# Weight tiles 64 and 96 bytes longer: moving the buffers of the split weights against the other operands in SBUF

## The chip, the cores and the metric

The kernel runs on one core of one Trainium2 chip. The metric is the device time of one execution in microseconds (us). The kernel before takes 2689.38 us, the median of 3 runs that lie between 2688.95 and 2689.45 us.

In what follows a matrix multiplication on TensorE is a *matmul*: one operand, the *weights* (128 columns here), is loaded into the array by an instruction of its own, the *weight load*; the other, the *moving* operand (up to 512 columns), streams past it, and the result is added up in a PSUM bank. The load of the next matmul's weights runs while the present matmul streams.

## The reference

A two-layer encoder trunk on 256 tokens of width 2048, in float32. Per layer:

```python
u = rmsnorm(x, norm_mix[l])
c_q, c_kv, k_pe, q_na, k_na, v_na, gate_a, gate_b = split(u @ w_in[l])      # 2048 x 8256
q  = (rmsnorm(c_q,  norm_qa[l])  @ w_uq[l])     # low-rank query and key/value of MLA
kv = (rmsnorm(c_kv, norm_kva[l]) @ w_ukv[l])
y_a = mla_attention(...) @ w_o_mla[l]           # 8 heads
y_b = neighbourhood_attention(...) @ w_o_na[l]  # 8 heads, windowed, with a bias
x = x + (sigmoid(gate_a) * y_a + sigmoid(gate_b) * y_b) @ w_out[l]
h = rmsnorm(x, norm_mlp[l]) @ w_ff1[l]          # 2048 -> 8192
x = x + square(relu(h)) @ w_ff2[l]              # 8192 -> 2048
```

and a last RMSNorm. Nearly all of the arithmetic is in the products of 256 rows with large weight matrices.

## The kernel before

**Two halves instead of float32.** Each float32 operand is split into `hi` (the value rounded to fp32r, a form that TensorE streams fast) and `lo` (what is left over, in fp32r too). A product is then hi·hi + hi·lo + lo·hi. Activations lie in *pairs*: one tile of 128 x 512 fp32r whose left 256 columns are the hi half and whose right 256 are the lo half. Weights come in by DMA as `raw` tiles (L167, 1 MB each, issued by SyncE), ScalarE casts them into a `hi` tile (L172), and VectorE subtracts to get the `lo` tile (L173). A `hi` or `lo` tile is 128 partitions x 1024 words, that is 4096 bytes in each partition, and holds two blocks of 128 x 512 of the weight matrix. There are four buffers for `hi` and four for `lo` (`HBUFS`), used in turn, three for `raw`.

**Two forms of product.** `gemm_b` (helper `mm_b`, L194 and L195) has the weight matrix in the array: the pair streams past a block of `hi` (512 columns, L194), then its left half past the same block of `lo` (256 columns, L195). `gemm_a` (helper `mm_a`, L199 to L201) has the activations in the array: `hi` streams past the pair's left block (L199), `lo` past the same block (L200), `hi` past the pair's right block (L201), 512 columns each. `gemm_b` makes q, k, the latents and the first half of the MLP; `gemm_a` the gates, the output projections and the second half of the MLP. A third helper, `mm_3` (L204 to L206), does the scores and the value products of the attention heads with 256 streaming columns. In the profile's names `bank<-pair,hi` reads: into a PSUM bank, moving operand pair, weights hi.

**What sets the order.** Each engine runs its list in program order; the tile framework puts the lists together with a timeline of its own, and starts an instruction where its buffers come free. Heads, rotations and transposes are generators that `tick` feeds in between the matmuls of the large products (`SPACING`, `LAG1`, `LAG2`). The ring `small` (8 buffers of 128 x 256) holds what `whole` (L210, L212) takes out of PSUM after a `gemm_b`, and a few short-lived tiles of the attention part.

**Where tiles lie.** Within a partition the pools stand one behind the other, and in a pool the buffers of one name: constants, the two `xt` tiles, `raw` (3 x 8192 bytes), `hi` (4 x 4096), `lo` (4 x 4096), the 44 slots of 2048 bytes (all pairs, and the value tiles `vh`, `vl`), then the small ones. In the built program every `raw`, `hi`, `lo` and slot buffer begins at a multiple of 256 bytes; `small` begins 64 bytes past one, and `pp`, the probabilities of a head that stream in the value product (L204 to L206, `abank<-pp,pair` and `abank<-pp,vh`), 192 bytes past one. The *distance* of a weight load below is the start of the tile that is loaded minus the start of the tile that streams meanwhile, modulo 256 bytes (the slices inside tiles begin at multiples of 512 bytes and change nothing in it). Before the change it is 0 for all loads of `mm_b` and `mm_a` and for the scores, and 64 for the loads beside a streaming `pp`.

Of the kernel before, what the change touches and what calls it, by code (L numbers as in the profile page):

```python
# [28 lines left out]
F32R = mybir.dt.float32r  # L29
# [4 lines left out]
P = 128  # L34
# [18 lines left out]

NSLOT, ABANKS, SMALL, RBUFS, HBUFS = 44, 3, 8, 3, 4


SPACING, LAG1, LAG2 = 6, 13, 3
# [3 lines left out]
def trunk(ctx: ExitStack, tc: tile.TileContext, x, w_in, w_uq, w_ukv, rpb, w_o_mla, w_o_na,  # L63
# [3 lines left out]
    wpool = ctx.enter_context(tc.tile_pool(name="wpool", bufs=4))  # L67
# [89 lines left out]
    def weights(w, nk, c0, n, before=None):  # L157


        step = 2 if before else 4  # L160
        for k0 in range(0, nk, 2):
            if before:
                before(k0)
            if k0 % step == 0:
                raw = wpool.tile([P, 2048], F32, tag="raw", name="raw", bufs=RBUFS)
                raw = raw[:, :step * n].rearrange("p (k n) -> p k n", n=n)
                nc.sync.dma_start(raw, w[k0 * P:(k0 + step) * P, c0:c0 + n].rearrange("(k p) n -> p k n", p=P))  # L167
            hi = wpool.tile([P, 1024], F32R, tag="hi", name="hi", bufs=HBUFS)
            lo = wpool.tile([P, 1024], F32R, tag="lo", name="lo", bufs=HBUFS)
            hi, lo = (t[:, :2 * n].rearrange("p (k n) -> p k n", n=n) for t in (hi, lo))  # L170
            src = raw[:, k0 % step:k0 % step + 2]
            nc.scalar.copy(hi, src)  # L172
            nc.vector.tensor_tensor(lo, src, hi.bitcast(F32), op=ALU.subtract)  # L173
            yield k0, hi, lo

    def weights_twice(w, nk, c0, n):

        raw = wpool.tile([P, 2048], F32, tag="raw", name="raw", bufs=RBUFS)
        raw = raw[:, :nk * n].rearrange("p (k n) -> p k n", n=n)
        nc.sync.dma_start(raw, w[:nk * P, c0:c0 + n].rearrange("(k p) n -> p k n", p=P))  # L180
        for k0 in range(0, nk, 8):
            hi = wpool.tile([P, 1024], F32R, tag="hi", name="hi", bufs=HBUFS)
            lo = wpool.tile([P, 1024], F32R, tag="lo", name="lo", bufs=HBUFS)
            hi, lo = (t.rearrange("p (k e n) -> p k e n", e=2, n=n) for t in (hi, lo))
            src = raw[:, k0:k0 + 8]
            for e in range(2):
                nc.scalar.copy(hi[:, :, e], src)
                nc.vector.tensor_tensor(lo[:, :, e], src, hi[:, :, e].bitcast(F32), op=ALU.subtract)
            hi, lo = (t.rearrange("p k e n -> p k (e n)") for t in (hi, lo))
            yield k0, hi, lo  # L190
# [24 lines left out]
    def gemm_a(w, c0, acts, evac):  # L215

        nk = len(acts)
        ps = [bank() for _ in range(2)]
        for k0, wh, wl in weights(w, nk, c0, 512):
            for t in range(2):  # L220
                for k in range(k0, k0 + 2):
                    mm_a(ps[t], have(acts, k), t, wh[:, k - k0], wl[:, k - k0], k == 0, k == nk - 1)
                tick()
        for t in range(2):
            evac(t, ps[t])

    def gemm_b(w, c0, acts, evac, before=None, ahead=None):

        nk = len(acts)
        ps = [bank() for _ in range(4)]  # L230
        for k0, wh, wl in weights(w, nk, c0, 512, before):
            for m in range(4):
                ms = slice(m * P, (m + 1) * P)
                for k in range(2):
                    mm_b(ps[m], wh[:, k, ms], wl[:, k, ms], have(acts, k0 + k), k0 + k == 0, k0 + k == nk - 1)
                tick()
        if ahead:
            ahead()
        for m in range(4):
            evac(m, ps[m])  # L240
# [234 lines left out]
    for l in range(DEPTH):  # L475
# [11 lines left out]
        for g in range(2):  # L487
            qn, kn = [None] * 4, [None] * 4
            gemm_b(wi, C_QN + g * 512, xg, to_pair(mix, qn), enter if l == g == 0 else None,
                   scaled if g == 0 else None)  # L490
            gemm_b(wi, C_KN + g * 512, xg, to_pair(mix, kn))
            ps = [bank() for _ in range(2)]
            for k0, wh, wl in weights(wi, NC, C_VN + g * 512, 512):
                for t in range(2):
                    for k in range(k0, k0 + 2):
                        mm_a(ps[t], xg[k], t, wh[:, k - k0], wl[:, k - k0], k == 0, k == NC - 1)
                    tick()
                    tick()
            vt = [values(ps[t], mix.col, t) for t in range(2)]
            for j in range(4):  # L500
                h = g * 4 + j
                queued.append(na_head(l, h, qn[j], kn[j], vt, setter(att_na, h)))
# [17 lines left out]
        for k0, wh, wl in weights_twice(wi, NC, C_KPE, ROPE):  # L520
            for k in range(8):
                mm_b(ps, wh[:, k], wl[:, k], xg[k0 + k], k0 + k == 0, k0 + k == NC - 1)
# [208 lines left out]
```

## Time and profile before

| | |
|---|---|
| median of 3 runs | 2689.38 us |
| the profiled execution: its own time | 2689.91 us |
| its span in the trace | 2688.1 us |
| TensorE busy with matmuls | 2666.8 us, 13596 instructions |
| weight loads | 2268.7 us, 13596 instructions |
| VectorE busy | 1602.9 us |
| ScalarE busy | 1277.1 us |

The span is 1.8 us shorter than the execution's own time, which also holds what lies around it. In the trace matmuls overlap: a matmul of 512 columns is recorded with some 390 ns, though the next one begins well before those are over. How fast the stream really runs is therefore read from the distance between the starts of neighbouring matmuls, or from how many of them begin in a window of known length, and not from the mean duration of one.

### The profile page before, as it was taken

How to read it: one execution, taken by the hardware profiler on the slowest of the kernel's cores; microseconds unless marked ns; L12 is line 12 of the kernel's file. 1: busy time of each engine (PE TensorE's matmuls, PEld its weight loads, DVE VectorE, ACT ScalarE, POOL GpSimd, SP SyncE). 2: the span in 40 equal slices, each digit the busy share in tenths (PEclk: the TensorE clock that was granted, in tenths of full speed). 3: DMA queues.
4: the chain of work that ended last, by engine and by line, in shares of the span. 5: the costliest groups of instructions: out<-in, count | busy, mean ns of one | idle time of the engine just before them, and what ended most of it. 6: DMA issues, size and time to landing. Idle time of an engine off the chain costs nothing.

```text
span 2688.1 us, 34037 instructions
## 1 busy us (share of the span) xinstructions
PE 2666.8 (99%) x13596; PEld 2268.7 (84%) x13596; DVE 1602.9 (60%) x2158; ACT 1277.1 (48%) x1815; POOL 60.5 (2%) x86
## 2 busy tenths in 40 slices
PE   8999999999999999999999999999999999999998
PEld 7888888888888888888888888888888888888886
DVE  5676486555655546556567754955556555565554
ACT  5554465444434434444445544644444344443443
POOL 1110000000000000000001100000000000000000
PEclk9999999999999999999999999999999999999999
DMA  7555644555565555555555555455555555655554
GB/s 231 184 165 189 195 161 155 189 184 180 186 203 186 190 190 186 197 193 189 183 183 179 171 187 183 153 167 188 188 188 188 189 187 194 208 189 193 188 188 141
DMA packets 253839, 496.49 MB, mean 185 GB/s; under 512 B 12688, under 2 KB 16784, under 8 KB 253680
## 3 DMA queue, kind: packets, MB, share of 16 engines
q1 hardware_dynamic: 250624, 488.14, 55.2%
q0 software_dynamic: 2048, 4.56, 0.6%
q8 instruction: 106, 1.74, 0.3%
q10 hardware_dynamic: 1008, 1.61, 0.2%
q14 instruction: 53, 0.43, 0.0%
HBM read 492.18 MB, written 2.10 MB: 184 GB/s over the span
## 4 chain that ended last, share of the span: by engine, by line
PE 84%; issue 14%; DVE 1%; DMA 1%; ACT 0%; POOL 0%; SPq 0%; POOLq 0%; DVEq 0%; ACTq 0%
PE bank L194 21%; PE bank L199 16%; PE bank L200 16%; PE bank L201 16%; PE bank L195 11%; DMA raw<-in_w_in 1%; PE abank L206 1%; PE abank L205 1%; PE abank L204 1%; PE abank L326 1%; PE abank L377 0%; DVE lo L173 0%; DVE wide L670 0%; PE abank L347 0%; ACT hi L172 0%
## 5 line engine op out<-in xcount | busy, mean ns | idle before, releaser
L173 DVE TENSOR_TENSOR lo<-raw,hi 128x1024 fp32r<-128x1024 f32 (+1 forms) x928 | 1132.5, 1222 | 977.8 <-ACT hi L172 973.0
L172 ACT CAST hi<-raw 128x1024 fp32r<-128x1024 f32 (+1 forms) x928 | 971.8, 1049 | 1131.1 <-PE bank L201 736.2
L194 PE MATMUL bank<-pair,hi 128*128 128x512 f32 x3008 | 1059.0, 398 | 2.3 <-DVE small L212 1.0
L200 PE MATMUL bank<-lo,pair 128*128 128x512 f32 (+1 forms) x2240 | 866.1, 387 | 0.0
L199 PE MATMUL bank<-hi,pair 128*128 128x512 f32 (+1 forms) x2240 | 865.8, 388 | 0.0
L201 PE MATMUL bank<-hi,pair 128*128 128x512 f32 (+1 forms) x2240 | 865.8, 387 | 0.0
L195 PE MATMUL bank<-pair,lo 128*128 128x256 f32 x3008 | 835.5, 280 | 0.4 <-DVE lo L173 0.3
L194 PEld LDWEIGHTS bank<-pair,hi 128*128 128x128 f32 x3008 | 563.5, 188 | 133.0 <-ACT hi L172 1.9
L195 PEld LDWEIGHTS bank<-pair,lo 128*128 128x128 f32 x3008 | 567.7, 189 | 5.9 <-DVE lo L173 1.6
L201 PEld LDWEIGHTS bank<-hi,pair 128*128 128x128 f32 x2240 | 420.8, 188 | 84.6
L199 PEld LDWEIGHTS bank<-hi,pair 128*128 128x128 f32 x2240 | 420.8, 188 | 84.1
L200 PEld LDWEIGHTS bank<-lo,pair 128*128 128x128 f32 x2240 | 420.9, 188 | 82.6
L150 ACT ACTIVATE pair<-small 128x256 fp32r<-128x256 f32 x200 | 73.6, 413 | 89.8 <-DVE small L641 67.1
L210 ACT COPY small<-bank 128x256 f32<-128x256 f32 x218 | 78.6, 369 | 29.0 <-PE bank L195 27.8
L152 DVE TENSOR_TENSOR pair<-small,pair 128x256 fp32r<-128x256 f32 x200 | 76.6, 418 | 19.2 <-ACT pair L150 19.2
L212 DVE TENSOR_TENSOR small<-bank,small 128x256 f32<-128x256 f32 x218 | 83.0, 416 | 0.2
L259 POOL TENSOR_TENSOR col<-var,mhalf 128x2 f32<-128x2 f32 x9 | 6.3, 702 | 1928.8 <-DVE var L257 1928.8
L619 DVE SCALAR_TENSOR_TENSOR xt<-bank,sq,xt 128x512 f32<-128x512 f32 x64 | 45.0, 744 | 7.8 <-PE bank L201 7.8
L641 DVE SCALAR_TENSOR_TENSOR small<-small 128x256 f32<-128x256 f32 x128 | 48.2, 418 | 0.0
L154 DVE SCALAR_TENSOR_TENSOR pair<-abank,g_sb,pair 128x256 fp32r<-128x256 f32 x64 | 29.2, 478 | 23.0 <-ACT pair L150 23.0
L150 ACT ACTIVATE pair<-abank,g_sb 128x256 fp32r<-128x256 f32 x64 | 28.2, 469 | 27.3 <-PE abank L326 23.4
L150 ACT ACTIVATE pair<-abank 128x256 fp32r<-128x256 f32 x64 | 23.6, 381 | 29.2 <-PE abank L206 19.1
(96 smaller groups left out, 789.9 us busy)
## 6 DMA issues: line engine op xcount, KB each, us to landing
raw<-in_w_ff SPq DMA_DIRECT2D x256, 1024.0 KB, 5.0
raw<-in_w_in SPq DMA_DIRECT2D x124, 1024.0 KB, 5.1
raw<-in_w_out SPq DMA_DIRECT2D x32, 1024.0 KB, 4.9
raw<-in_w_o_na SPq DMA_DIRECT2D x16, 1024.0 KB, 4.9
raw<-in_w_o_mla SPq DMA_DIRECT2D x16, 1024.0 KB, 4.9
raw<-in_w_ukv SPq DMA_DIRECT2D x8, 1024.0 KB, 4.9
raw<-in_w_uq SPq DMA_DIRECT2D x8, 768.0 KB, 4.6
raw<-in_w_in SPq DMA_DIRECT2D x10, 512.0 KB, 4.9
```

The costliest lines, as they stand in the source:

```text
L150: nc.scalar.activation(dst[:, :S], src, AF.Copy, scale=scale)
L152: nc.vector.tensor_tensor(dst[:, S:], src, dst[:, :S].bitcast(F32), op=ALU.subtract)
L172: nc.scalar.copy(hi, src)
L173: nc.vector.tensor_tensor(lo, src, hi.bitcast(F32), op=ALU.subtract)
L194: nc.tensor.matmul(ps, wh, a, start=first, stop=False)
L195: nc.tensor.matmul(ps[:, :S], wl, a[:, :S], start=False, stop=last)
L199: nc.tensor.matmul(ps, a[:, t * P:(t + 1) * P], wh, start=first, stop=False)
L200: nc.tensor.matmul(ps, a[:, t * P:(t + 1) * P], wl, start=False, stop=False)
L201: nc.tensor.matmul(ps, a[:, S + t * P:S + (t + 1) * P], wh, start=False, stop=last)
L210: nc.scalar.copy(h, ps[:, S:])
L212: nc.vector.tensor_tensor(t, ps[:, :S], h, op=ALU.add)
L641: nc.vector.scalar_tensor_tensor(t, t, 0.0, t, op0=ALU.max, op1=ALU.mult)
```

## The change

The tiles `hi` and `lo` are allocated 16 and 24 words longer (64 and 96 bytes in each partition), and only their first 1024 words are used. So the second buffer of `hi` begins 64 bytes later relative to the 256-byte grid than the first, and so on; the same with 96 for `lo`. The room comes from the ring `small`, which has 7 buffers instead of 8. No instruction is added, taken away or changed in size.

```diff
-NSLOT, ABANKS, SMALL, RBUFS, HBUFS = 44, 3, 8, 3, 4
+NSLOT, ABANKS, SMALL, RBUFS, HBUFS = 44, 3, 7, 3, 4
+
+HPAD, LPAD = 16, 24
...
-            hi = wpool.tile([P, 1024], F32R, tag="hi", name="hi", bufs=HBUFS)
-            lo = wpool.tile([P, 1024], F32R, tag="lo", name="lo", bufs=HBUFS)
+            hi = wpool.tile([P, 1024 + HPAD], F32R, tag="hi", name="hi", bufs=HBUFS)[:, :1024]
+            lo = wpool.tile([P, 1024 + LPAD], F32R, tag="lo", name="lo", bufs=HBUFS)[:, :1024]
```

The same two lines change in `weights` and in `weights_twice`. In the built programs the starts of the buffers, modulo 256 bytes, are:

| buffers | before | after |
|---|---|---|
| `raw` 0 to 2 | 0, 0, 0 | 0, 0, 0 |
| `hi` 0 to 3 | 0, 0, 0, 0 | 0, 64, 128, 192 |
| `lo` 0 to 3 | 0, 0, 0, 0 | 0, 96, 192, 32 |
| the 44 slots (pairs, `vh`, `vl`) | 0 | 128 |
| `small` | 64 | 192 |
| `pp` | 192 | 64 |

From these follow the distances, for the buffers 0 to 3 in turn:

| load | while this streams | before | after |
|---|---|---|---|
| `hi` (`mm_b`) | pair | 0, 0, 0, 0 | 128, 192, 0, 64 |
| `lo` (`mm_b`) | pair | 0, 0, 0, 0 | 128, 224, 64, 160 |
| pair (`mm_a`) | `hi` | 0, 0, 0, 0 | 128, 64, 0, 192 |
| pair (`mm_a`) | `lo` | 0, 0, 0, 0 | 128, 32, 192, 96 |
| pair (`mm_3`, scores) | pair | 0 | 0 |
| `vh`, `vl`, pair (`mm_3`, values) | `pp` | 64 | 64 |

The order of the instructions stays as it is but for one place in each layer: the projections of the latents into the heads of MLA (`w_uq`, `w_ukv`), where the framework works with one `small` buffer less. In the large products the lists of TensorE are alike row for row. Here is a piece in the first half of the MLP, TensorE, before:

```order
L194 MATMUL bank_9941<-pair_5128,hi_9965 128x512
L195 MATMUL bank_9941<-pair_5128,lo_9966 128x256
L194 MATMUL bank_9942<-pair_5125,hi_9965 128x512
L195 MATMUL bank_9942<-pair_5125,lo_9966 128x256
L194 MATMUL bank_9942<-pair_5128,hi_9965 128x512
L195 MATMUL bank_9942<-pair_5128,lo_9966 128x256
```

and the same rows after (lines of the file are two further down):

```order
L196 MATMUL bank_9941<-pair_5128,hi_9965 128x512
L197 MATMUL bank_9941<-pair_5128,lo_9966 128x256
L196 MATMUL bank_9942<-pair_5125,hi_9965 128x512
L197 MATMUL bank_9942<-pair_5125,lo_9966 128x256
L196 MATMUL bank_9942<-pair_5128,hi_9965 128x512
L197 MATMUL bank_9942<-pair_5128,lo_9966 128x256
```

Nothing moved: 512 columns past a block of `hi`, then 256 past the block of `lo`, in both.

In the MLA projections rows do move. VectorE in layer 0, before (L212 takes a product out of PSUM, L351 is the rotation of the query, L402 scales a product by the row of the norm, L362 belongs to a head's softmax):

```order
L212 TENSOR_TENSOR small<-bank,small 128x256
L152 TENSOR_TENSOR pair<-abank,pair 128x256
L351 TENSOR_TENSOR small<-small 128x256
L402 TENSOR_TENSOR small<-small,rrow 128x256 x2
L362 TENSOR_SCALAR nms<-nmx 128x2
L402 TENSOR_TENSOR small<-small,rrow 128x256
L173 TENSOR_TENSOR lo<-raw,hi 128x1024 x2
L380 TENSOR_TENSOR pp<-abank,pp 128x2x256
```

and the same place after:

```order
L353 TENSOR_TENSOR small<-small 128x256
L404 TENSOR_TENSOR small<-small,rrow 128x256
L214 TENSOR_TENSOR small<-bank,small 128x256
L404 TENSOR_TENSOR small<-small,rrow 128x256
L364 TENSOR_SCALAR nms<-nmx 128x2
L175 TENSOR_TENSOR lo<-raw,hi 128x1024
L404 TENSOR_TENSOR small<-small,rrow 128x256
L175 TENSOR_TENSOR lo<-raw,hi 128x1024
```

The removal of one product from PSUM (L214, L212 before) now stands behind the rotation and one scaling, where before it stood ahead of both; the splits of weights (L175) come a place or two earlier or later. TensorE's own list is shifted at the same places, by whole groups of matmuls that change places with each other; none is added.

More of the change, by code (lines that the diff above doesn't have):

```diff
@@ L181, in weights_twice @@
         for k0 in range(0, nk, 8):
-            hi = wpool.tile([P, 1024], F32R, tag="hi", name="hi", bufs=HBUFS)
-            lo = wpool.tile([P, 1024], F32R, tag="lo", name="lo", bufs=HBUFS)
+            hi = wpool.tile([P, 1024 + HPAD], F32R, tag="hi", name="hi", bufs=HBUFS)[:, :1024]
+            lo = wpool.tile([P, 1024 + LPAD], F32R, tag="lo", name="lo", bufs=HBUFS)[:, :1024]
             hi, lo = (t.rearrange("p (k e n) -> p k e n", e=2, n=n) for t in (hi, lo))
```

## The prediction

> **What bounds the kernel now.** First the head of the page: span, busy engines, granted clock.
>
> ```profile
> span 2688.1 us, 34037 instructions
> PE 2666.8 (99%) x13596; PEld 2268.7 (84%) x13596; DVE 1602.9 (60%) x2158; ACT 1277.1 (48%) x1815; POOL 60.5 (2%) x86
> PEclk9999999999999999999999999999999999999999
> PE 84%; issue 14%; DVE 1%; DMA 1%; ACT 0%; POOL 0%; SPq 0%; POOLq 0%; DVEq 0%; ACTq 0%
> ```
>
> TensorE is busy throughout, at full granted clock, and holds the chain that ended last. The view of waits says that it is not starved:
>
> ```profile
> PE abank L326 <- DMA xt<-in_x: 7.4, 3, 4.5
> PE bank L194 <- DVE small L212: 1.0, 2, 0.5
> PE bank L194 <- ACT hi L172: 1.0, 2, 0.7
> ```
>
> Ten of 2688 us. What is left is the pace of the matmul stream itself, and of the two ways to read it only the distance between starts counts (durations overlap). Who carries the stream is in the groups by line and shape:
>
> ```profile
> L194 PE MATMUL bank<-pair,hi 128*128 128x512 f32 x3008 | 1059.0, 398 | 2.3 <-DVE small L212 1.0 <-ACT hi L172 1.0 <-DVE pair L154 0.3
> L200 PE MATMUL bank<-lo,pair 128*128 128x512 f32 x2176 | 848.0, 390 | 0.0
> L201 PE MATMUL bank<-hi,pair 128*128 128x512 f32 x2176 | 847.7, 390 | 0.0
> L199 PE MATMUL bank<-hi,pair 128*128 128x512 f32 x2176 | 847.3, 390 | 0.0
> L195 PE MATMUL bank<-pair,lo 128*128 128x256 f32 x3008 | 835.5, 280 | 0.4 <-DVE lo L173 0.3
> ```
>
> So 3008 pairs of `mm_b` (512 + 256 columns) and three lines of `mm_a` with 2176 matmuls of 512 columns each, 6528 in all. Their pace, from two windows of TensorE, one inside a `gemm_a` stretch and one inside `gemm_b`:
>
> ```profile
> 920.00:990.00 70.00, 70.00 (x310) 1.00 0.59 195
> 1010.00:1080.00 70.00, 70.00 (x402) 1.00 0.56 184
> ```
>
> The counts are of the matmuls touched by the window, one or two more than begin in it: `mm_a` starts every 70.00 / 309 = 226.5 ns, and `mm_b` every 70.00 / 400 = 175 ns, that is 350 ns a pair. A run of scores in `mm_3`, 256 columns each, at distance 0 like all of these:
>
> ```profile
> 365.38 0.28 PE L205 MATMUL abank<-pair 128*128 128x256 f32 x1
> ...
> 366.58 0.28 PE L206 MATMUL abank<-pair 128*128 128x256 f32 x1
> ```
>
> Ten starts in 1.20 us: 120 ns each. Between 512 columns (226.5) and 256 (120) lie 106.5 ns, so a column costs 0.416 ns; 512 columns are 213 ns and 768 are 319.5. What each matmul pays beyond its columns is 13.5 ns in `mm_a`, about 30.5 ns a pair in `mm_b`, and 13.5 ns in the scores. Over the kernel that is 6528 x 13.5 = 88 us and 3008 x 30.5 = 92 us. **These 180 us are all that a better placement can return**; no wait and no other engine is in the way of returning them.
>
> **Does the distance between operands matter?** One place of the trace before has another distance than 0: the value products, where `pp` streams while `vh`, `vl` or a pair is loaded, distance 64.
>
> ```profile
> 428.95 0.28 PE L205 MATMUL abank<-pp,pair 128*128 128x256 f32 x1
> 429.06 0.28 PE L206 MATMUL abank<-pp,pair 128*128 128x256 f32 x1
> 429.18 0.28 PE L204 MATMUL abank<-pp,pair 128*128 128x256 f32 x1
> 429.29 0.28 PE L205 MATMUL abank<-pp,pair 128*128 128x256 f32 x1
> 429.40 0.28 PE L206 MATMUL abank<-pp,pair 128*128 128x256 f32 x1
> 429.52 0.39 PE L201 MATMUL bank<-hi,pair 128*128 128x512 f32 x1
> ```
>
> Five starts in 0.57 us: 114 ns each, 6 ns less than the scores with the same shape, helper and type. It is the only row that speaks for the change; the runs are short (five or six matmuls), so part of it may be work pushed onto the next matmul.
>
> The second thing to see is that the pace at distance 0 isn't one number. Two stretches of `mm_b` with the same tiles and shapes:
>
> ```profile
> 36.25 0.40 PE L194 MATMUL bank<-pair,hi 128*128 128x512 f32 x1
> ...
> 37.98 0.39 PE L194 MATMUL bank<-pair,hi 128*128 128x512 f32 x1
> ```
>
> ```profile
> 1004.85 0.40 PE L194 MATMUL bank<-pair,hi 128*128 128x512 f32 x1
> ...
> 1006.97 0.40 PE L194 MATMUL bank<-pair,hi 128*128 128x512 f32 x1
> ```
>
> The first holds five pairs in 1.73 us, 346 ns each, the second six in 2.12 us, 353 ns each. The same instructions can fall into a faster or a slower rhythm. And `mm_a`, right after the value products above:
>
> ```profile
> 430.44 0.39 PE L199 MATMUL bank<-hi,pair 128*128 128x512 f32 x1
> 430.66 0.39 PE L200 MATMUL bank<-lo,pair 128*128 128x512 f32 x1
> 430.89 0.39 PE L201 MATMUL bank<-hi,pair 128*128 128x512 f32 x1
> 431.12 0.39 PE L199 MATMUL bank<-hi,pair 128*128 128x512 f32 x1
> ```
>
> From 429.52 to 430.44 four matmuls take 0.92 us, 230 ns each; the next three 0.68 us, 226.7 ns. After a disturbance `mm_a` needs a few matmuls at 230 before it is back at 226.5. A change of distance at every new buffer is such a disturbance.
>
> **The change, part by part.** Nothing is added or removed, so the terms are paces times counts, against the profiled execution's 2689.9 us (span 2688.1; the median of the runs is 0.5 us lower).
>
> *Loads in `mm_b`.* All 3008 loads of `lo` come to a distance other than 0, and of the 3008 of `hi` three quarters, 2256 (the third buffer has 0 again): 5264 loads. Price of one: the nearest row is the value product's, -6 ns. Bounds: nothing (if only 64 helps, or the rhythm decides), and -15 ns (the whole 30.5 ns of a pair, halved). I take -6: 5264 x 6 = **-31.6 us**. Ends: 0 and -79 us.
>
> *Loads in `mm_a`.* While `hi` streams (4352 matmuls) three quarters, 3264, while `lo` streams all 2176: 5440 loads. No row shows a 512-column matmul at another distance. Bounds: the same -6 ns, 5440 x 6 = -33 us, and on the other side the disturbed pace: 230 instead of 226.5 on all 6528 matmuls, +23 us. I take **0**: 226.5 is already the best pace that a long stretch of this trace shows, its surplus of 13.5 ns is no larger than the scores', and loss and gain are about alike. Both ends stay for the range.
>
> *One `small` buffer less and the moved rows.* In the large products TensorE's list is the same. In the MLA projections, a stage where VectorE is the fullest:
>
> ```profile
> 345.00:420.00 75.00, 74.49 (x471) 67.05 (x470) 65.53 (x143) 46.87 (x104) 0.00 (x0) 1.00 0.49 158
> L212 DVE TENSOR_TENSOR small<-bank,small 128x256 f32<-128x256 f32 x218 | 83.0, 416 | 0.2
> ```
>
> VectorE (third busy figure) has 65.5 of 75 us, and TensorE idles half a microsecond. A PSUM removal that comes behind two further VectorE instructions is late by 2 x 0.42 us; behind it on VectorE stand the splits of the weights, and TensorE waits for both the bank and the `lo` tile. If none of that were covered it would be 0.8 us for each of the four groups of heads in each of two layers: +6.7 us. TensorE has other heads' matmuls to put in between, and its waits there are 1.0 us in total now, so I take **0**; below nothing it cannot go by more than the 1.0 us.
>
> *DMAs, ScalarE, VectorE elsewhere.* `raw` keeps its place, so the DMAs land as before. The casts and subtractions write the same 1024 words at other starts; no row shows whether starts matter to them, but both engines are under 61% busy, and the splits run ahead of the matmuls (TensorE's wait for `hi` is 1.0 us in the whole run). Taken at 0.
>
> Sum: 2689.9 - 31.6 + 0 + 0 = **2658 us**, 1.2% less.
>
> A rule of the skill speaks against the whole change: the Trainium skill, SBUF — State Buffer, "Who interferes with whom", gives TensorE two independent read ports, one for the moving operand and one for weight loads, and says "PE and ACT never wait on anyone". By it the starts of the buffers can't matter, and the sum would be 2690. The trace does not quite agree: same shape, 114 against 120 ns. But it has only one distance to show.
>
> **The rivals.**
>
> *Everything gains (15%).* `mm_a` takes the -6 ns too: 2658 - 33 = 2625 us. For it: `mm_a` and the scores have the same surplus of 13.5 ns, and the scores' falls at distance 64. Against: that surplus may be fixed by the load alone.
>
> *Nothing (14%).* 2690 us. The 114 ns would then be an effect of neighbours, not of distance: short runs between other shapes. The two rhythms of `mm_b` at equal distance speak for it: pace varies by 7 ns a pair with no change of address. This is also where the skill's rule ends.
>
> *The rhythm of `mm_a` is lost (33%), slower.* A weight tile serves 12 matmuls of `gemm_a` before the next buffer comes, now with other distances, and within them `hi` and `lo` differ as well. If the disturbed pace becomes the normal one, `mm_a` goes from 226.5 to 230 ns, +23 us; if `mm_b` at the same time settles at 353 instead of 350 ns a pair, 3008 x 3 = +9 us: 2690 + 32 = 2722 us, and 2713 us with `mm_a` alone. For it: 226.5 holds today only because every load has one distance. Against: it came back within four matmuls after the value products. It decides the sign when it costs more than `mm_b` gains, that is from 31.6 / 6528 = 4.8 ns a matmul on if `mm_b` gains in full, and from any loss over 0.8 ns (0.2% of the time) if `mm_b` gains nothing.
>
> *That it doesn't do what it says* can only be partly so: one `hi` buffer in four keeps distance 0, which is in the counts.
>
> **How the numbers follow.** `mm_b` gains and `mm_a` holds: 38%, with 2641 to 2679 as its own range (half of `mm_a`'s loads gaining as well; a third of the price on `mm_b`). Everything gains: 15%, around 2625. Nothing: 14%, around 2690. Slower: 33%, around 2713 to 2722. Faster by over 0.2% (5.4 us, about what a measurement of this kernel can tell from no change): 0.53; within: 0.14; slower: 0.33. The range 2620 to 2722 leaves out a part of the first rival, with the far end of the price on `mm_b` (-79 us), and the upper part of the last, under 2 in 10.
>
> **What would show it.** The two windows of the same length: over 309 starts in 70 us for `mm_a` means that it gained, under 305 that the rhythm went; over 403 in `gemm_b` means that the price is right (350 - 10.5 ns a pair gives 412). Right is the step on distances if the pace differs from buffer to buffer, by stretches of 12 matmuls in `gemm_a` and 8 pairs in `gemm_b`; wrong if all four buffers run alike. TensorE's waits for L214 and for `hi` and `lo` should stay at a few us; tens of them would mean that the lost `small` buffer, not the placement, set the time. The forecast fails if the 6 ns belong to the distance 64 alone or to the neighbours of the value products, or if `mm_a` can't hold its rhythm.

## The result, and the profile after

The changed kernel takes 2720.28 us (median of 4 runs, 2719.99 to 2720.6) against 2689.28 us of the kernel before: the ratio is 1.0115, with a 95% interval of 1.0098 to 1.0133. It is slower by 31 us. The time lies in the range, but the likeliest case, 2658 us, had the wrong sign; what came is the third rival, which stood at 2713 to 2722 us. Of all executions told of below, one of the 256-byte control took 6068.98 us at the same clock and is left out of its ratio.

The head of the page after:

```profile
span 2718.7 us, 34033 instructions
PE 2696.8 (99%) x13596; PEld 2273.6 (84%) x13596; DVE 1602.3 (59%) x2158; ACT 1274.1 (47%) x1815; POOL 62.3 (2%) x86
PEclk9999999999999999999999999999999999999999
PE 84%; issue 14%; DVE 1%; DMA 1%; ACT 0%; POOL 0%; SPq 0%; POOLq 0%; DVEq 0%
```

The span is 30.6 us longer, and TensorE's busy time by 30.0 us, with the same 13596 matmuls at the same full clock. VectorE and ScalarE are as busy as before. The view of TensorE's waits after (us in total, times, longest):

```profile
PE abank L328 <- DMA xt<-in_x: 7.4, 3, 4.3
PE bank L196 <- ACT hi L174: 1.4, 2, 0.8
PE bank L196 <- DVE small L214: 1.1, 2, 0.5
```

TensorE waits 10.5 us in all, against 10.0 before. So the time went into the pace of the stream, and the two windows of the prediction, at the same places of the program, say into which half of it (busy us and count of matmuls, then clock, DMA share, GB/s; `mm_a` first, `mm_b` second):

```profile
930.00:1000.00 70.00, 70.00 (x303) 1.00 0.57 194
1020.00:1090.00 70.00, 70.00 (x404) 1.00 0.57 188
```

302 starts of `mm_a` in 70 us where there were 309: 231.8 ns instead of 226.5. That is below the 305 that the prediction named for a lost rhythm. `mm_b` has 404 instead of 402, both counted with the one or two that had begun before the window; a full gain would have brought some 12 more. The groups by line and shape show the same two things in their recorded durations:

```profile
L196 PE MATMUL bank<-pair,hi 128*128 128x512 f32 x3008 | 1055.2, 395 | 2.7 <-ACT hi L174 1.4 <-DVE small L214 1.1 <-DVE pair L156 0.3
L202 PE MATMUL bank<-lo,pair 128*128 128x512 f32 x2176 | 859.9, 395 | 0.0
L201 PE MATMUL bank<-hi,pair 128*128 128x512 f32 x2176 | 858.2, 395 | 0.0
L203 PE MATMUL bank<-hi,pair 128*128 128x512 f32 x2176 | 857.3, 394 | 0.0
```

The three lines of `mm_a` went from 390 ns to 394 and 395, the 512-column line of `mm_b` from 398 to 395. A longer look at the stream in `mm_a`:

```profile
929.81 0.40 PE L202 MATMUL bank<-lo,pair 128*128 128x512 f32 x1
930.05 0.39 PE L203 MATMUL bank<-hi,pair 128*128 128x512 f32 x1
930.27 0.39 PE L201 MATMUL bank<-hi,pair 128*128 128x512 f32 x1
930.50 0.40 PE L202 MATMUL bank<-lo,pair 128*128 128x512 f32 x1
930.74 0.39 PE L203 MATMUL bank<-hi,pair 128*128 128x512 f32 x1
930.97 0.40 PE L201 MATMUL bank<-hi,pair 128*128 128x512 f32 x1
931.20 0.39 PE L202 MATMUL bank<-lo,pair 128*128 128x512 f32 x1
931.43 0.40 PE L203 MATMUL bank<-hi,pair 128*128 128x512 f32 x1
931.67 0.39 PE L201 MATMUL bank<-hi,pair 128*128 128x512 f32 x1
931.90 0.40 PE L202 MATMUL bank<-lo,pair 128*128 128x512 f32 x1
```

Nine starts in 2.09 us, 232 ns each, with no gap that stands out: each matmul is a little late, not a few of them much.

**The account.** If the time from each matmul's start to the next one's is booked on the form of the first of the two, the sums add up to the whole run. I use these sums for all kernels below; they are worked out from all starts of a trace (a number in brackets counts the matmuls; the last of the 6528 `mm_a` has none behind it). *Distance* means addresses from here on, and never time:

| sum of the times from start to start, us | before | after | |
|---|---|---|---|
| `mm_a` (6527) | 1485.5 | 1519.8 | +34.3 |
| `mm_b` (6016) | 1063.5 | 1059.5 | -4.0 |
| all other matmuls | 123.0 | 123.3 | +0.3 |
| first to last matmul | 2672.1 | 2702.6 | +30.5 |

### The profile page after: what moved, and what is told of

It reads as the page before. It is cut to its first block, busy times and chain, and to the rows that moved or that the text cites. A ratio compares the mean times of both kernels' runs of the same rounds, so it can differ in the third digit from the quotient of the medians.

```text
span 2718.7 us, 34033 instructions
## 1 busy us (share of the span) xinstructions
PE 2696.8 (99%) x13596; PEld 2273.6 (84%) x13596; DVE 1602.3 (59%) x2158; ACT 1274.1 (47%) x1815; POOL 62.3 (2%) x86
## 4 chain that ended last, share of the span: by engine, by line
PE 84%; issue 14%; DVE 1%; DMA 1%; ACT 0%; POOL 0%; SPq 0%; POOLq 0%; DVEq 0%
PE bank L196 21%; PE bank L202 17%; PE bank L201 17%; PE bank L203 16%; PE bank L197 11%; DMA raw<-in_w_in 1%; PE abank L206 1%; PE abank L207 1%; PE abank L208 1%; PE abank L328 1%; PE abank L379 0%; DVE lo L175 0%; DVE wide L672 0%; PE abank L349 0%; ACT hi L174 0%
## 5 line engine op out<-in xcount | busy, mean ns | idle before, releaser
L175 DVE TENSOR_TENSOR lo<-raw,hi 128x1024 fp32r<-128x1024 f32 (+1 forms) x928 | 1132.2, 1221 | 1006.2 <-ACT hi L174 1004.6
L202 PE MATMUL bank<-lo,pair 128*128 128x512 f32 (+1 forms) x2240 | 877.9, 392 | 0.0
L201 PE MATMUL bank<-hi,pair 128*128 128x512 f32 (+1 forms) x2240 | 876.5, 392 | 0.0
L203 PE MATMUL bank<-hi,pair 128*128 128x512 f32 (+1 forms) x2240 | 875.2, 391 | 0.0
L212 ACT COPY small<-bank 128x256 f32<-128x256 f32 x218 | 79.6, 370 | 28.5 <-PE bank L197 27.5
L214 DVE TENSOR_TENSOR small<-bank,small 128x256 f32<-128x256 f32 x218 | 83.2, 414 | 0.2
L152 ACT ACTIVATE pair<-abank,g_sb 128x256 fp32r<-128x256 f32 x64 | 28.4, 470 | 27.7 <-PE abank L328 23.8
```

Of the source, the lines that this page charges most:

```text
L152: nc.scalar.activation(dst[:, :S], src, AF.Copy, scale=scale)
L201: nc.tensor.matmul(ps, a[:, t * P:(t + 1) * P], wh, start=first, stop=False)
L202: nc.tensor.matmul(ps, a[:, t * P:(t + 1) * P], wl, start=False, stop=False)
L203: nc.tensor.matmul(ps, a[:, S + t * P:S + (t + 1) * P], wh, start=False, stop=last)
L212: nc.scalar.copy(h, ps[:, S:])
L214: nc.vector.tensor_tensor(t, ps[:, :S], h, op=ALU.add)
```

## The experiments

The theories. *A price for each load:* a load costs what its distance costs, and the changed kernel pays a mean of such prices. *The rhythm:* any one distance is as good as 0, and what costs is that the distance changes from load to load and from buffer to buffer. *The ring:* the lost `small` buffer does it. Times are medians, ratios are against the kernel before on the same chip (2689.3 to 2689.5 us in every set).

### The ring of small tiles alone

```diff
-NSLOT, ABANKS, SMALL, RBUFS, HBUFS = 44, 3, 8, 3, 4
+NSLOT, ABANKS, SMALL, RBUFS, HBUFS = 44, 3, 7, 3, 4
```

> The kernel before with 7 small buffers in place of 8 and no padding: all distances stay 0, only the moved rows in the MLA projections are new. Theory RHYTHM (the pace of mm_a is held by equal distances from matmul to matmul and is lost when they vary) and theory PRICE (each distance other than 0 has its own higher price in mm_a): both 2690 us, within 3 us. Rival RING (the lost small buffer costs): 2700 us or more, with TensorE waits on L212 of tens of us.

Measured: 2689.11 us, ratio 0.9999 (0.999 to 1.0008). The ring costs nothing, and the moved rows in the MLA projections neither. The same stage of the kernel *after* says so as well (five busy times in the order PE, PEld, DVE, ACT, POOL):

```profile
350.00:425.00 75.00, 74.45 (x471) 66.82 (x470) 66.17 (x146) 46.18 (x105) 0.00 (x0) 1.00 0.49 153
```

471 matmuls in 75 us, as many as before. All that follows is about where the tiles lie.

### One distance for all loads: 64, 128, 192

Three kernels with the ring of 7, tiles of 1024 words as before, and one small unused tile between `lo` and the slots, which pushes all slots on by 64, 128 or 192 bytes. Every load of `mm_a` then has that distance, every load of `mm_b` 256 bytes minus it, and nothing changes from buffer to buffer. The 64 bytes:

```diff
+            if not spare:
+                spare.append(wpool.tile([P, 16], F32, tag="spare", name="spare", bufs=1))
+                nc.vector.memset(spare[0], 0.0)
```

> As e1_small7, with one unused tile of 64 bytes between lo and the slots: every load of mm_a is at distance 64, every load of mm_b at 192, for all buffers alike (an added memset of the unused tile is once, under 1 us). RHYTHM: mm_a again steady near 226.5 ns, time 2690 us within 10 us. PRICE: mm_a near 232 ns a matmul as in the changed kernel, 2715 to 2725 us. If distance 64 has the price of the value products (114 in place of 120 ns), less: 2650 us.

> As e2_all64 with 128 bytes: all loads of mm_a and mm_b at distance 128. RHYTHM: 2690 us within 10 us. PRICE: 2715 to 2725 us, or another steady value that belongs to 128.

> As e2_all64 with 192 bytes: mm_a at distance 192, mm_b at 64. RHYTHM: 2690 us within 10 us. PRICE: 2715 to 2725 us; if only the distance matters and 64 is cheap, mm_b gains here and mm_a in e2_all64.

Measured: 2732.15 us (1.0158, 1.0143 to 1.0173), 2726.68 us (1.0138, 1.0122 to 1.0155) and 2709.45 us (1.0074, 1.0059 to 1.0089). All three are slower, two of them slower than the change itself, though the distance never changes in them. The rhythm alone is refuted as the cause. Two windows of the kernel before, one in `gemm_a` and one in `gemm_b`:

```profile
745.00:810.00 65.00, 65.00 (x288) 1.00 0.58 195
1015.00:1075.00 60.00, 60.00 (x345) 1.00 0.57 185
```

the same two with all slots 64 bytes on (distance 64 in the first, 192 in the second):

```profile
745.00:810.00 65.00, 65.00 (x280) 1.00 0.56 185
1015.00:1075.00 60.00, 60.00 (x343) 1.00 0.56 184
```

and with 192 bytes (distance 192 in the first, 64 in the second):

```profile
745.00:810.00 65.00, 65.00 (x285) 1.00 0.60 198
1015.00:1075.00 60.00, 60.00 (x342) 1.00 0.56 185
```

279 starts in 65 us instead of 287: 233.0 ns for `mm_a` at distance 64, against 226.5. And `mm_b` at distance 64, where the prediction took 6 ns a load off, has *fewer* starts than before.

### A control: 256 bytes

The same tile with 64 words, which moves everything as the others did but leaves all distances at 0 modulo 256.

> As e2_all64 with an unused tile of 256 bytes: everything behind lo lies 256 bytes further on, so all distances are 0 modulo 256 as before. If only the distance modulo 256 counts: 2689 us within 1 us, and mm_a at 226.5 ns. If the shift itself, or a distance modulo 512 or more, counts: a few us to some tens more, as with 64, 128 and 192.

Measured: 2689.26 us, ratio 1.0000 (0.9988 to 1.0012). The spare tile, its one extra instruction and the shift as such cost nothing. For a shift by 256 bytes the distance modulo 256 is thus all that counts; no longer shift was tried in this way.

### Other distances: 32 and 224

The spare tile with 8 and with 56 words.

> As e2_all64 with 32 bytes: mm_a at distance 32, mm_b at 224, all buffers alike. PRICE (each distance has its own steady pace, 0 the best for mm_a): slower than 2690; if the price grows with the distance from 0, between 2690 and 2732 us; the 234 ns that the lo matmuls at distance 32 take in the changed kernel, taken for all of mm_a, would give 2690 + 6528 x 7.5 ns = 2739 us.

> As e2_all64 with 224 bytes: mm_a at distance 224, mm_b at 32. PRICE: 192 was the cheapest of the three shifts (2709 us), so 224, which is nearer to 0 from below, between 2690 and 2709 us. If mm_b has a better distance than 0, this is one of the two left to see it.

Measured: 2720.91 us (1.0118, 1.0088 to 1.0147) and 2736.93 us (1.0177, 1.0148 to 1.0207). The second was expected between 2690 and 2709 us: the price does not fall steadily towards 0. `mm_a` is slow in both, but `mm_b` differs. The window in `gemm_b`, first with its loads at 224 (slots 32 bytes on):

```profile
1015.00:1075.00 60.00, 60.00 (x348) 1.00 0.56 188
```

then at 32 (slots 224 bytes on):

```profile
1015.00:1075.00 60.00, 60.00 (x342) 1.00 0.54 183
```

348 against 345 before and 342. Distance 224 is a gain for `mm_b`: 1053.7 us in the sum instead of 1063.5.

### Buffers that differ, but one distance for hi and lo

The changed kernel with equal paddings. `hi` and `lo` of one buffer then have the same distance, so that the three loads of a triple agree, and only the buffers differ (0, 64, 128, 192).

```diff
-HPAD, LPAD = 16, 24
+HPAD, LPAD = 16, 16
```

> The changed kernel with both pads at 64 bytes: hi and lo of one buffer number have the same start, so within one weight tile (12 matmuls of mm_a) all loads have one distance, and it goes 0, 192, 128, 64 over the four buffers. PRICE alone: mm_a is the mean of the four steady paces, (226.7 + 228.9 + 232.6 + 233.4) / 4 = 230.4 ns, time 2690 + 6528 x 3.7 ns = 2714 us. RHYTHM on top (the pace needs some matmuls to settle after each change of distance): more than that, up to the 2720 us of the changed kernel; the stretches at distance 0 then show the slow pace too.

Measured: 2715.81 us (1.0099, 1.0069 to 1.0128). `mm_a` has a mean of 1511.8 / 6527 = 231.6 ns; the mean of the four kernels with one distance each (0, 64, 128, 192: 1485.0, 1526.6, 1521.6 and 1498.9 us) is 231.1. So the prices by distance explain nearly all, and the change from buffer to buffer adds half a nanosecond. Here the weights are shifted and the slots are not, the other way round than in the kernels with one distance, and the paces agree: whole weight tiles have a median of 232.9, 232.7 and 229.3 ns at 64, 128 and 192, against 233.4, 232.6 and 229.0. Those at distance 0 have a mean of 228.6 instead of 226.9 ns. One of them shows where that comes from:

```profile
751.68 0.39 PE L201 MATMUL bank<-hi,pair 128*128 128x512 f32 x1
...
752.83 0.39 PE L203 MATMUL bank<-hi,pair 128*128 128x512 f32 x1
...
754.42 0.40 PE L201 MATMUL bank<-hi,pair 128*128 128x512 f32 x1
```

Five matmuls in 1.15 us, 230 ns each, then seven in 1.59 us, 227 ns. The fast pace is back after about five of twelve; the mean over all 113 such tiles shows the same.

### The best pair of distances: 0 for gemm_a, 224 for gemm_b

`hi` and `lo` tiles of 1088 words (4352 bytes, 17 x 256), of which `gemm_b`, `weights_twice` and the projections of `w_uq` and `w_ukv` use 1024 words from 224 bytes on, and `gemm_a` those from the start; six small tiles to make room.

```diff
+AT_B, AT_A = 56, 0
...
-    def weights(w, nk, c0, n, before=None):
+    def weights(w, nk, c0, n, before=None, at=AT_A):
...
+            hi = wpool.tile([P, 1088], F32R, tag="hi", name="hi", bufs=HBUFS)[:, at:at + 1024]
+            lo = wpool.tile([P, 1088], F32R, tag="lo", name="lo", bufs=HBUFS)[:, at:at + 1024]
...
-        for k0, wh, wl in weights(w, nk, c0, 512, before):
+        for k0, wh, wl in weights(w, nk, c0, 512, before, AT_B):
```

Its control has `AT_B, AT_A = 0, 0`.

> A version made from the steady paces: weight tiles of 4352 bytes (17 x 256, so all buffers start alike), the products of gemm_b and the latents written 224 bytes into the tile (mm_b at distance 224, 347.0 ns a pair in e6_all32), those of gemm_a at its start (mm_a at distance 0, 226.5 ns); 6 small buffers to make room. PRICE (each distance has its steady pace, and settling after a change takes about five matmuls): mm_b 3008 x (351.5 - 347.0) = -13.5 us, mm_a as before: 2676 us, a little more for the settling between stretches. If paces don't carry over to another arrangement, or 6 small buffers cost: 2689 us or more.

> The control of e9_b224: the same tile lengths and 6 small buffers, all written at their start, so every distance is 0 modulo 256 as before. 2689 us within 2 us; if the ring of 6 costs, some us more, which e9_b224 would then carry too.

Measured: 2679.77 us, ratio 0.9964 (0.995 to 0.9978), and 2689.65 us, ratio 1.0001 (0.9991 to 1.001), for the control. This version beats both kernels, by 9.5 us against the one before. Its page and its windows:

```profile
span 2677.9 us, 34035 instructions
PE 2654.2 (99%) x13596; PEld 2272.5 (85%) x13596; DVE 1603.0 (60%) x2158; ACT 1276.6 (48%) x1815; POOL 61.5 (2%) x86
```

```profile
745.00:810.00 65.00, 65.00 (x288) 1.00 0.58 194
1015.00:1075.00 60.00, 60.00 (x347) 1.00 0.59 193
```

`mm_a` is where it was (1484.8 us in the sum), `mm_b` went from 1063.5 to 1054.3 us, and that is nearly the whole gain; it is less than the 13.5 us that the steady paces had promised. Here the weights are shifted by 224 bytes and the slots are not, in the kernel with the slots 32 bytes on it is the other way round; `mm_b` comes to 1054.3 and 1053.7 us. So it is the distance between the two operands that counts, as with the equal paddings, and not where one of them begins.

### Further distances

The same kernel with `AT_B, AT_A = 60, 60` (`mm_b` at 240, `mm_a` at 16), `24, 4` (96 and 240) and `4, 40` (16 and 96); one execution each.

> As e9_b224 with both forms written 240 bytes into the tile: mm_b at distance 240, mm_a at 16, a step of 16 bytes that no run has shown. If the price of mm_a jumps with any distance other than 0: near 233 ns a matmul, 2725 us or so. If it grows from 0 on: between 227 and 233 ns. mm_b: 347 ns a pair if 240 is like 224, 351 if like 0.

> As e9_b224 with gemm_b written 96 bytes in (mm_b at distance 96) and gemm_a 16 bytes in (mm_a at 240). mm_a: 227 to 233 ns, near 233 if it jumps; mm_b: no forecast, one of 347 to 354 ns a pair as for the other distances.

> As e9_b224 with gemm_b written 16 bytes in (mm_b at distance 16) and gemm_a 160 bytes in (mm_a at 96). mm_a at 96: between 229 and 237 ns as at the other distances but 0, so slower than 2690 us together; if 96 were as good as 0, 227 ns. mm_b at 16: 347 to 354 ns a pair.

Measured: 2749.72, 2710.86 and 2726.19 us. None beats 0 for `mm_a`; 16 and 96 are as good for `mm_b` as 224.

### Two distances within a triple

`hi` of `gemm_a` at distance 0, `lo` at 192, the same in all buffers (and `mm_b` at 160). The edit is shown against the kernel with the best pair.

```diff
-AT_B, AT_A = 56, 0
+AT_B, AT_A, AT_LO = 40, 0, 16
...
+            lo = lo[:, AT_LO:AT_LO + 1024] if at == AT_A else lo[:, at:at + 1024]
```

> As e9_b224, but in gemm_a the lo tile is written 64 bytes in and hi at the start: mm_a's loads are at distance 0 while hi streams and at 192 while lo streams, for all buffers alike, as in the third buffer of the changed kernel; gemm_b is written 160 bytes in. PRICE taken load by load: (2 x 226.7 + 228.9) / 3 = 227.4 ns a matmul in mm_a. If the pace belongs to the sequence of three loads: a steady value of its own, near the 231.7 ns that the third buffer's stretches show in the changed kernel. mm_b at 160: one of 347 to 354 ns a pair, no forecast.

Measured: 2721.21 us, one execution. By prices `mm_a` would run at two thirds of 226.7 and one third of 229.0, 227.5 ns. It runs at 232.0 ns throughout (1517.8 us in the sum), slower than either distance alone. Three groups of this kernel:

```profile
L204 PE MATMUL bank<-hi,pair 128*128 128x512 f32 x2176 | 857.9, 394 | 0.0
L203 PE MATMUL bank<-lo,pair 128*128 128x512 f32 x2176 | 857.4, 394 | 0.0
L202 PE MATMUL bank<-hi,pair 128*128 128x512 f32 x2176 | 857.2, 395 | 0.0
```

The two lines that keep distance 0 are recorded as long as the one with 192, and as long as the three lines of the changed kernel. A price for each load by itself is refuted too: the pace belongs to the sequence of loads.

### All distances in one table

Sums over the whole trace, as in the account above, and the pace of twelve `mm_a` in a row or six pairs of `mm_b` that is kept in long stretches:

| distance | `mm_a`, us | steady, ns | `mm_b`, us | steady, ns a pair |
|---|---|---|---|---|
| 0 | 1484.8 to 1485.5 | 226.7 | 1063.1 to 1064.1 | 347 and 353 |
| 16 | 1543.5 | 237, some 233 | 1053.3 | 347 |
| 32 | 1526.4 | 233.4 | 1069.9 | 353 |
| 64 | 1526.6 | 233.4 | 1069.4 | 353 |
| 96 | 1532.4 | 234.3 | 1053.9 | 347 |
| 128 | 1521.6 | 232.6 | 1062.9 | 351 |
| 160 | | | 1063.4 | 350 |
| 192 | 1498.9 | 229.0 | 1065.5 | 349 and 353 |
| 224 | 1526.6 | 233.4 | 1053.7 (1054.3) | 347 |
| 240 | 1515.7 | 231.7 | 1065.7 | 353, some 347 |

The rest of each kernel, 122.0 to 123.8 us, hardly moves.

## Why the prediction was wrong

**Right: what bounds the kernel.** TensorE, by its pace, at full clock, with a few us of waits. Every run's time followed the two sums of its stream.

**Right: the ring, the moved rows, the DMAs, VectorE and ScalarE at 0.** The ring alone gave -0.2 us.

**Wrong: -6 ns for each load of `mm_b`, -31.6 us in all. Measured: -4.0 us.** Two things failed in this step. First the price itself. I read it from one run of five value products at 114 ns. The trace before has 58 runs of value products, 26 of them of a single matmul. In the others 116.7 ns lie between two starts, ten steps of over 200 ns left out, and in the scores 119.2 ns, four of 306 ns left out: 2.5 ns, not 6, while single steps lie between 113 and 124. With the long steps in, the value products are not faster at all (123.2 against 122.2). Second, and worse, what the value products show isn't a property of distance 64 that other forms share: with every load of `mm_b` at 64 it is slower than at 0, by 1069.4 - 1063.5 = 5.9 us. At the distance from which the price was read it had the wrong sign for the form to which it was carried. Why the value products run a little faster stays open. The -4.0 us that did come don't follow from the sums of the table either: weighted by the changed kernel's distances they give +0.3 us. In its trace whole weight tiles of `mm_b` take 347 to 349 ns a pair in three of the four buffers and 351 where `hi` and `lo` both have 128 (medians; 352 before). Why the mixture helps `mm_b` and hurts `mm_a`, no run separates.

**Wrong: `mm_a` at 0, with +23 us as the worst. Measured: +34.3 us.** This is the step that set the sign. I argued that 226.5 ns could hardly get better, which is true of every distance tried, and that loss and gain were about alike, which doesn't follow from it: a stream at its best can only lose. That its surplus of 13.5 ns equals that of the scores says nothing: the price of a column was taken from the difference of just these two, so both surpluses had to come out alike. By the steady paces of the table the changed kernel's distances have a mean of 231.05 ns (two thirds on 128, 64, 0, 192 while `hi` streams, one third on 128, 32, 192, 96 while `lo` streams), (231.05 - 226.7) x 6528 = +28.4 us. The other 6 us are what the two distances within a triple and the change of buffers add, if paces and additions may be summed in this way; the runs with equal paddings (0.5 ns) and with two distances (232.0 instead of 227.5) show that both exist.

**The rival of the lost rhythm: right in place and sign, with a reason that is half right.** It gave +23 us for `mm_a` and +9 us for `mm_b`; measured are +34.3 and -4.0, so that its 2722 us came close through two misses that cancel. "226.5 holds today only because every load has one distance" is not enough: every load has one distance at 64, too, and the pace there is 233.4. It holds because that distance is 0.

**The test by buffers.** The prediction said that the step on distances is right if the buffers differ. In the changed kernel they hardly do in `mm_a`: 231.5 to 232.7 ns while `hi` streams, and the buffer with distance 0 has 231.9 (while `lo` streams, 231.4 to 234.3, the highest at 32). The test was badly chosen, since a buffer's pace carries on into the next and the `lo` load within a triple spoils that of `hi`. Kernels with one distance throughout were needed to see what a distance does.

**"These 180 us are all that a better placement can return."** A bound, and far too wide: the best placement found returns 10 of them, nearly all in `mm_b`. In no run does `mm_a` keep a steady pace below 226.7 ns, some 13.5 ns beyond the 213 that the prediction estimates for its columns; no placement that was tried touches that part.

**The rule against the change.** By the Trainium skill, SBUF — State Buffer, "Who interferes with whom", TensorE's two read ports are independent and it waits on nobody. The runs disagree with what the prediction read in that, namely that starts can't matter: with the same matmuls, times between 2679.77 and 2749.72 us are to be had by the starts of buffers alone.

## What to carry to other kernels

Where TensorE runs without waits, count the starts in a window before and after a change of layout; recorded durations overlap, and TensorE's busy share stays at 99% whichever pace it has. Move all loads of one form of product to one distance first, so that what a distance does can be read without the effect of a mixture, and choose the distance for each form by itself: here 0 is best for the form with the activations in the array, and 16, 96 or 224 for the one with the weights. A price read from a run of five short matmuls is not the pace of a long stream of another form.

## What the runs showed that I had not expected

The start of a loaded tile against the start of the streaming one, modulo 256 bytes, changes the pace of `mm_a` by over 4% (226.7 to about 237 ns) with no wait in the trace. Shifts of 16 bytes already matter (1543.5 us at 16, 1485.5 at 0), and 256 don't.

Many of the steady paces lie in steps of some 6.7 ns: three matmuls of `mm_a` take 680, 687 or 700 ns (3 x 226.7, 229.0 and 233.4) at 0, 192 and 32, 64 or 224, and a pair of `mm_b` 347 or 353 ns. The paces at 16, 96, 128, 160 and 240 show that not all do. The same instructions at the same distance can keep either of two paces. Of the 2583 stretches of six pairs before the change (one from each pair on, so that they overlap), 926 ran at 347 ns a pair and 1195 at 353, to the nearest ns; with `mm_b` at 224 and `mm_a` at 0, 2082 of 2569 ran at 347 and none at 353. That is where the distances 16, 96 and 224 gain.

What makes one distance fast and another slow, no run here separates. It stays open, and so does whether a distance that wasn't tried does better.
